# A streaming encoder step on one core: the order of the first loads (frames, rows of vectors, weights, the second block's frames)

## The chip, the cores and the metric

The kernel runs on one core of one Trainium2 chip. The metric is the device time of one execution in microseconds; of several runs the median is given. Beside it stands a profile of one execution. Its engines: TensorE (PE, with the weight loads as PEld), VectorE (DVE), ScalarE (ACT), GpSimd (POOL) and SyncE (SP), which here only issues DMAs.

## The reference

One layer of a hybrid encoder on 2048 prompt frames and 32 sample frames of 1024 channels, all float32:

```python
hn = rmsnorm(h, g_mix)
proj = hn @ w_in                       # 1024 x 3072: hA, bA, cA, zA, vB, zB of 512 columns each
yA = bA * causal_conv3(cA * hA) * silu(zA)
yB = pool_mix(vB) * silu(zB)           # trailing means over 2, 4, 8, 16 frames, a linear map, a scale
h = h + concat(yA, yB) @ w_out
gate = sigmoid(rmsnorm(h, g_ple) @ w_ple_gate)
y = rmsnorm(h + (p @ w_ple) * gate, g_final)
```

It also returns the last rows of u = cA * hA and of vB as states.

## The kernel before

**Tiling.** The 2080 frames are cut into five blocks of 416 columns (NB): three tiles of 128 frames and one short tile of 32. A tile is loaded (`x_load`, L405), its squares are summed on ScalarE (`sumsq`, L91), GpSimd makes the root (`rstd_of`, L69), VectorE normalizes it, TensorE transposes it (`turn`, L426), and what comes out of PSUM is split in two: ScalarE casts the upper part (hi), VectorE subtracts it for the lower part (lo). A product is three matmuls a piece: hi by hi, hi by lo, lo by hi. Weights of `w_in` are split in the same way: `raw_weight` (L524) loads 1024 x 128 columns, 512 KB, in pieces of 512 bytes, and casts and subtractions make hi and lo.

**The beginning** is written out by hand for the first block, with an order that the scheduler must keep where `in_turn` or `later=True` stands. SyncE first issues g_mix's row, the three frame tiles of the first block (L628) and the short tile, which holds the last 32 frames of block 0 and of block 1 in two loads (L629). `first_normal` (L634) normalizes by halves, with g_mix spread over the partitions in two PSUM tiles, `pg`, and not yet in the SBUF tile g_bc. `first_hi` and `first_lo` (L659, L663) write the pieces. VectorE's order is fixed: tile 0 and tile 1 normalized, the first lo piece, tile 2 and the short tile normalized, one hi piece, then the lo pieces. `fill` (L388) puts idle transposes on TensorE in between.

**The first weights** are zb, v and c of the first 128 columns: zb loaded at L689, v and c in `other_first` (L706). `first_products` (L599) runs three rounds of 24 matmuls over the three of them (hi by hi, hi by lo, lo by hi), and steps `second_block` (L726) forward in between. That generator takes block 1's three tiles (`x_tile`, L731: load and squares), normalizes them with g_bc (L424), transposes them, splits them into B's pieces "12" and "22" and forms the sums of blocks that the later groups' products need (T1, T2, T3, and T4, which goes to memory).

**The rows.** Small vectors (conv weights and bias, pool scale, the two caches, g_ple) are loaded as rows of one tile (L768 to L775, six loads), transposed once (L777) and kept as `vec`. Then pool_w is loaded and split (L788). The tile's memset is GpSimd's.

**Queues and buffers.** All these loads go through SyncE's one queue in the order of issue. Completion is told by eight semaphores taken in turn, so a load is issued once the load eight places ahead of it has landed. Frame tiles live in a pool of five buffers (`xin`), raw weights in one of four (`raws`: zb, v, c, pool_w; raw_h of `weights("h", ...)`, the next one, takes zb's buffer when VectorE has read it). What is not fixed by hand is put in order by a scheduler when the program is built: each engine has one list and works through it strictly in order.

SyncE's list in the beginning: g_mix, tiles 0, 1, 2, short tile (two), zb, v, c, six rows, pool_w, block 1's tiles 0, 1, 2, raw_h, raw_za, raw_b, raw_zbv.

Of the kernel before, what the change touches and what calls it, by code (L numbers as in the profile page):

```python
# [15 lines left out]
P = 128  # L16
D = 1024
KC = D // P
# [16 lines left out]
def trunk(ctx, tc, x_p, x_s, c_conv, c_pool, p_p, p_s, g_mix, w_in, conv_w, conv_b, pool_w,  # L35
          pool_scale, w_out, g_ple, w_gate, w_ple, g_fin, y_p, y_s, sc_p, sp_p, sc_s, sp_s):
    nc = tc.nc
# [53 lines left out]
    def sumsq(x, n, name, r=None, later=False):  # L91
        ssq = sm.tile([P, 1], F32, tag="ssq", name=f"ssq_{name}")
        ins = nc.scalar.activation(junk[:n], x[:n], AF.Square, accum_out=ssq[:n])  # L93
        if later:
            tc.keep_in_program_order(ins)
        return rstd_of(ssq, n, name, r)
# [207 lines left out]
    def slot(name):  # L304
        return acts[0].tile([P, SLOT], F32R, tag="hn", name=name)
# [13 lines left out]
    def ring4(t, name):  # L319
        return t.tile([P, D], F32, tag="t", name=name)  # L320
# [21 lines left out]
    with ExitStack() as s1:  # L342
# [21 lines left out]
        def ftile(name):  # L364
            return wk.tile([P, KH, P], F32, tag="f", bufs=4, name=name)
# [33 lines left out]
        def x_rows(tb, c):  # L399
            r = tb * NB + c * P  # L400
            if c < 3:
                return x_p[r:r + P]
            return x_p[r:r + DEC] if tb < 4 else x_s

        def x_load(name, rows):  # L405

            t, at = ring4(xin, f"xt_{name}"), 0
            for src in rows:
                m = src.shape[0]
                nc.sync.dma_start(t[at:at + m], src)  # L410
                at += m
            return t, at, f"x{name}"

        def x_stat(x, later=False):

            t, n, name = x
            return t, n, sumsq(t, n, name, later=later)

        def x_tile(name, rows):
            return x_stat(x_load(name, rows))  # L420

        def normal(x):
            xt, n, r = x
            nc.vector.scalar_tensor_tensor(xt[:n], xt[:n], r[:n], g_bc[:n], op0=ALU.mult, op1=ALU.mult)  # L424

        def turn(x, half, name, get=tbank, later=False):  # L426
            xt, n, _ = x
            pt = get(name)
            for k in range(KH):
                kk = half * KH + k  # L430
                ins = nc.tensor.transpose(pt[:, k * P:k * P + n], xt[:n, kk * P:(kk + 1) * P], ident[:n, :n])
                if later:
                    tc.keep_in_program_order(ins)
            return pt.rearrange("p (k t) -> p k t", k=KH)[:, :, :n]
# [68 lines left out]
        def six(g):  # L503

            B = {}
            for i, names in enumerate(SLOTS):
                t = slot(f"B{g}_{i}")
                B.update((q, piece_of(t, c)) for c, q in enumerate(names))
            return B
# [11 lines left out]
        raw_ring = lambda name: raws.tile([P, KC, P], F32, tag="t", name=name)  # L521
        spare_ring = lambda name: xin.tile([P, KC, P], F32, tag="t", name=name)

        def raw_weight(kind, j, name, ring=raw_ring):  # L524
            t = ring(f"raw_{name}")
            col = cols[kind] * WA + j * P
            raw_loads.append(nc.sync.dma_start(t, w_in[:, col:col + P].rearrange("(k p) n -> p k n", p=P)))
            return t

        raw_loads = []  # L530
# [95 lines left out]

        B0 = {}
        ahead0 = [x_load(f"0_{c}", [x_rows(0, c)]) for c in range(3)]  # L628
        short0 = x_load("0_3", [x_rows(0, 3), x_rows(1, 3)])  # L629
        B0.update(six(0))  # L630
        def in_turn(ins):
            tc.keep_in_program_order(ins)
# [26 lines left out]
        def first_hi(c, half, copy=nc.scalar.copy):  # L659
            hi, _, src = place0(c, half)  # L660
            in_turn(copy(hi, src))
# [9 lines left out]
                fill((2, 3, 2)[c], short_bank)  # L671


        for c in range(3):
            first_x.append(x_stat(ahead0[c], True))
        first_tile(0)
# [9 lines left out]
        first_hi(2, 0)  # L686
        first_tile(3)
        first_hi(2, 1, nc.vector.tensor_copy)
        raw = raw_weight("zb", 0, "firstzb")  # L689
        first_zb = [wtile(f"w_firstzb_{half}") for half in range(2)]  # L690
        for half, t in enumerate(first_zb):
            in_turn(nc.scalar.copy(t[:, :, 0], raw[:, half * KH:half * KH + KH]))
# [11 lines left out]
        first_los = {}  # L704

        def other_first(kind):  # L706
            raw = raw_weight(kind, 0, f"first{kind}")
            ts = [wtile(f"w_first{kind}_{half}") for half in range(2)]
            for half, t in enumerate(ts):
                nc.scalar.copy(t[:, :, 0], raw[:, half * KH:half * KH + KH])  # L710

            def los():
                for half, t in enumerate(ts):
                    nc.vector.tensor_tensor(t[:, :, 1], raw[:, half * KH:half * KH + KH], t[:, :, 0].bitcast(F32),
                                            op=ALU.subtract)

            first_los[kind] = los
            return ts

        first_w.extend(other_first(kind) for kind in ("v", "c"))  # L720
        for half in range(2):
            nc.scalar.copy(g_bc[:, half * NH:half * NH + NH], pg[half])
# [3 lines left out]
        def second_block():  # L726

            spans = [(c, slice(c * P, min(NB, c * P + P))) for c in range(4)]
            xs = []
            for c in range(3):  # L730
                x = x_tile(f"1_{c}", [x_rows(1, c)])  # L731
                normal(x)
                xs.append((x, slice(0, P)))
                yield
            xs.append((short0, slice(DEC, 2 * DEC)))
            whole = []
            for c, cs in spans:
                x, ts = xs[c]

                turned = x[0].rearrange("p (k t) -> p k t", k=KC)[:, :, :ts.stop - ts.start]  # L740
                for half, q in enumerate(("12", "22")):
                    pt = turn(x, half, f"pt1_{c}_{half}", bank)[:, :, ts]
                    put(B0[q][:, :, :, cs], pt)
                    nc.scalar.copy(turned[:, half * KH:half * KH + KH], pt)
                whole.append((turned[:, :KH], turned[:, KH:]))
                yield
            op = lambda o, a, b, op=ALU.subtract: nc.vector.tensor_tensor(o, a, b, op=op)
            for c, cs in spans:
                p12, p22 = whole[c]
# [12 lines left out]
                to_memory(p_d["T4"], f"T4_0_{c}", t4, c * P, n)  # L762
                yield

        second = second_block()


        rows = ftile("rows").rearrange("p k n -> p (k n)")[:112, :P]  # L768
        nc.gpsimd.memset(rows, 0.0)
        nc.sync.dma_start(rows[0:12], conv_w[0].rearrange("r (j c) -> (r j) c", c=P))  # L770
        nc.sync.dma_start(rows[12:16], conv_b[0].rearrange("(j c) -> j c", c=P))
        nc.sync.dma_start(rows[16:20], pool_scale[0].rearrange("(j c) -> j c", c=P))
        nc.sync.dma_start(rows[32:40], c_conv[0, 0].rearrange("r (j c) -> (r j) c", c=P))
        nc.sync.dma_start(rows[40:100], c_pool[0, 0].rearrange("r (j c) -> (r j) c", c=P))
        nc.sync.dma_start(rows[100:108].rearrange("k (q c) -> k q c", q=4), g_ple[0].rearrange("(q k c) -> k q c", q=4, k=KC))  # L775
        pv = tbank("pv")
        nc.tensor.transpose(pv[:, :112], rows, ident[:112, :112])  # L777
        vec = const.tile([P, 112], F32, name="vec")
# [492 lines left out]
        for gi, tbs in enumerate(GROUPS):  # L1271
            if gi == 2:

                frames_in.close()
                t = slot("hn_4")
# [40 lines left out]
    with ExitStack() as s2:  # L1316
# [113 lines left out]
        for i in range(0, NT - 1, 2):  # L1430
            with tc.issue_after(loaded[-1].ins):
                x = [load_rows(xh, "x", i + b, x_p) for b in range(2)] if i else [first_x, second_x]
# [4 lines left out]
            if last:  # L1437
                n = tiles[NT - 1][1]
# [6 lines left out]
            if last:  # L1445
                x = load_rows(xh, "x", NT - 1, x_p, x_s)
# [34 lines left out]
        for k in range(KH):  # L1481
            raw = [ring4(t, f"wg_r{k}_{i}") for i, t in enumerate(((ya, ya), (ya, xh), (xh, xh), (ya, ya))[k])]
# [243 lines left out]
        n = tiles[NT - 1][1]  # L1726
# [47 lines left out]
```

## Time and profile before

| what | us |
|---|---|
| median of 3 runs | 921.37 |
| lowest and highest | 920.61, 921.42 |
| the profiled execution | 921.02 |
| its span in the profile | 919.2 |
| mean granted TensorE clock in the span | 0.997 |

How the views read. The stages give, for each stretch of the span, the busy time and number of instructions of PE, PEld, DVE, ACT and POOL, then the granted clock, the share of the DMA engines and GB/s. The chain of waits is the work that ended last, followed back: start, duration, engine, tile or group and line. The timeline gives start, busy time, engine, line, operation, output and inputs, shapes, count, and in brackets the idle time just ahead with what ended it. "SPq" is SyncE's queue: its time is the issue, not the transfer. In the list of DMA issues the last number is the time from issue to landing. Line numbers are those of the kernel before.

### The profile page before, as it was taken

The page shows a single profiled execution, that of the slowest core. Times are in us where ns is not written, and L with a number is a line of the kernel's source. Part 1 is how long each engine was busy: PE and PEld are TensorE (multiplying, and loading weights), DVE is VectorE, ACT ScalarE, POOL GpSimd, SP SyncE. Part 2 cuts the span into 40 slices and gives each one's busy share as a digit, 9 for nine tenths or more (in the row PEclk, how much of TensorE's full clock was granted, in tenths as well). Part 3 has the DMA queues.
Part 4 walks back from the last instruction along what each step waited for, and adds up shares of the span by engine and source line. Part 5 has one row for each costly group of instructions (what it writes and reads, how often), then busy time and mean ns, then how long its engine had stood idle before and what let it go on. Part 6 is the DMA issues. An engine that isn't in the chain of part 4 may idle for free.

```text
span 919.2 us, 13202 instructions
## 1 busy us (share of the span) xinstructions
PE 905.7 (99%) x4529; PEld 822.7 (90%) x4529; DVE 722.4 (79%) x1236; ACT 481.2 (52%) x894; POOL 159.8 (17%) x307
## 2 busy tenths in 40 slices
PE   8999999999999999999999999999999999999996
PEld 6999999999999999999999987888878878888885
DVE  6996989999576989795777679665558658889885
ACT  7744565654445555443545356334336755555554
POOL 3111222121000333210000120111203301111113
PEclk9999999999999999999999999999999999999998
DMA  9357687798945898638975469865777984676564
GB/s 262 93 145 217 168 249 230 234 294 287 413 131 168 251 227 225 216 122 296 274 228 173 155 243 291 267 189 177 237 228 231 354 263 143 203 242 235 188 209 169
DMA packets 138447, 205.12 MB, mean 223 GB/s; under 512 B 13116, under 2 KB 101724, under 8 KB 137101
## 3 DMA queue, kind: packets, MB, share of 16 engines
q1 hardware_dynamic: 117773, 139.41, 48.9%
q0 software_dynamic: 17872, 59.45, 19.8%
q10 hardware_dynamic: 2736, 5.44, 1.8%
q8 instruction: 35, 0.57, 0.3%
q14 instruction: 31, 0.25, 0.1%
HBM read 136.60 MB, written 67.64 MB: 222 GB/s over the span
## 4 chain that ended last, share of the span: by engine, by line
PE 91%; DVE 3%; DMA 2%; ACT 2%; issue 1%; POOL 0%; SPq 0%; POOLq 0%; DVEq 0%; ACTq 0%
PE x_g L175 9%; PE x_o L175 9%; PE x_zab L591 7%; PE x_zbv L591 6%; PE x_ch L591 5%; PE z_g L175 5%; PE e L107 4%; PE z_o L175 4%; PE z_zab L591 3%; PE h L591 3%; PE z_zbv L591 3%; PE z_ch L591 3%; PE b L591 3%; PE za L591 3%; PE zb L591 2%; PE c L591 2%
## 5 line engine op out<-in xcount | busy, mean ns | idle before, releaser
L80 ACT CAST y_S<-y_fS 128x512 fp32r<-128x512 f32 x32 | 19.5, 622 | 42.2 <-PE x_o L175 20.4
L175 PE MATMUL x_g<-wg_b,g_S 128*128 128x512 f32 x128 | 35.7, 389 | 0.0
L175 PE MATMUL x_o<-wo_b,y_S 128*128 128x512 f32 x128 | 35.6, 390 | 0.0
L591 PE MATMUL x_zab<-B,w_zab_S 128*128 128x416 f32 x168 | 34.2, 352 | 0.2 <-ACT V L987 0.2
L591 PE MATMUL z_zab<-B,w_zab_S 128*128 128x416 f32 x168 | 34.3, 351 | 0.0
L591 PE MATMUL x_zbv<-B,w_zbv_S 128*128 128x416 f32 x168 | 34.2, 352 | 0.0
L591 PE MATMUL z_ch<-B,w_ch_S 128*128 128x416 f32 x168 | 34.1, 351 | 0.0
L591 PE MATMUL z_zbv<-B,w_zbv_S 128*128 128x416 f32 x168 | 34.0, 351 | 0.0
L591 PE MATMUL x_ch<-B,w_ch_S 128*128 128x416 f32 x168 | 34.0, 351 | 0.0
L107 PE MATMUL e<-wq,pps 128*128 128x512 f32 x144 | 33.1, 390 | 0.0
L591 PEld LDWEIGHTS x_zab<-B,w_zab_S 128*128 128x128 f32 x168 | 31.3, 188 | 0.9 <-ACT V L987 0.5
L107 PEld LDWEIGHTS e<-wq,pps 128*128 128x128 f32 x144 | 27.0, 188 | 5.6
L591 PEld LDWEIGHTS z_zbv<-B,w_zbv_S 128*128 128x128 f32 x168 | 31.4, 188 | 0.3
L591 PEld LDWEIGHTS x_ch<-B,w_ch_S 128*128 128x128 f32 x168 | 31.4, 188 | 0.3
L591 PEld LDWEIGHTS z_ch<-B,w_ch_S 128*128 128x128 f32 x168 | 31.3, 188 | 0.3
L591 PEld LDWEIGHTS z_zab<-B,w_zab_S 128*128 128x128 f32 x168 | 31.3, 188 | 0.3
L591 PEld LDWEIGHTS x_zbv<-B,w_zbv_S 128*128 128x128 f32 x168 | 31.3, 188 | 0.4
L1542 DVE SCALAR_TENSOR_TENSOR h<-h,rstd_f,g_bc 128x1024 f32<-128x1024 f32 (+1 forms) x15 | 19.3, 1284 | 14.0 <-POOL rstd_f L76 14.0
L80 ACT CAST y<-y 128x512 fp32r<-128x512 f32 x24 | 14.8, 618 | 29.4 <-PE z_o L175 12.8
L1335 DVE TENSOR_TENSOR c_o<-x_o,x 128x512 f32<-128x512 f32 x14 | 9.7, 691 | 25.7 <-PE x_o L175 25.7
L72 POOL TENSOR_SCALAR ms_f<-ssq_f 128x1 f32<-128x1 f32 (+1 forms) x15 | 6.6, 441 | 128.8 <-ACT junk L93 128.5
L175 PEld LDWEIGHTS x_o<-wo_b,y_S 128*128 128x128 f32 x128 | 23.9, 188 | 5.2 <-ACT c_o L1340 0.3
(591 smaller groups left out, 2694.9 us busy)
## 6 DMA issues: line engine op xcount, KB each, us to landing
y<-y_d SPq DMA_DIRECT2D x16, 512.0 KB, 6.0
x<-in_x_prompt_dram SPq DMA_DIRECT2D x16, 512.0 KB, 6.0
h_d<-x SPq DMA_DIRECT2D x16, 512.0 KB, 4.3
h<-h_d SPq DMA_DIRECT2D x16, 512.0 KB, 3.5
xt<-in_x_prompt_dram SPq DMA_DIRECT2D x15, 512.0 KB, 7.8
e<-e_d SPq DMA_DIRECT2D x15, 512.0 KB, 5.2
out_dram<-h POOLq DMA_DIRECT2D x14, 512.0 KB, 3.0
p_dT<-T POOLq DMA_DIRECT2D x12, 512.0 KB, 6.0
```

What stands on the lines that cost most here:

```text
L72: nc.gpsimd.tensor_scalar(ms[:n], ssq[:n], scalar1=1.0 / D, scalar2=EPS, op0=ALU.mult, op1=ALU.add)
L80: ins = nc.scalar.copy(hi, src)
L107: nc.tensor.matmul(ps, pps[:, a, k], wp[k][b][:, cs], start=k + q == 0, stop=k == 1 and q == 2)
L175: nc.tensor.matmul(ps[:n], lhs[:, k, a, :n], w[b][:, k], start=start and k + q == 0, stop=k == KH - 1 and q == 2, skip_group_check=True)
L591: nc.tensor.matmul(ps[:, :NB], lhs[:, k, x], b[:, k, y], start=start and k + q == 0, stop=stop and k == KH - 1 and q == 2, skip_group_chec ...
L1335: add = lambda o, a, b: nc.vector.tensor_tensor(o, a, b, op=ALU.add)
L1542: nc.vector.scalar_tensor_tensor(h[:n], h[:n], rf[:n], g_bc[:n], op0=ALU.mult, op1=ALU.mult)
```

## The change

- The three frame tiles' loads are kept in a list, and `third_landed` is the third one's load.
- The rows' tile, its memset and five of its six loads move up, to right behind the frames' loads. The sixth (g_ple) stands behind block 1's first tile.
- The loads of zb, v and c are issued together, behind them. zb's gets an added dependency on the third frame tile's load.
- Block 1's first tile is loaded right behind c; tiles 1 and 2 are loaded when v and c are made, ahead of pool_w. `second_block` takes the tiles so loaded instead of loading them.

```diff
+        frame_loads = []
...
-                nc.sync.dma_start(t[at:at + m], src)
+                frame_loads.append(nc.sync.dma_start(t[at:at + m], src))
...
-        def raw_weight(kind, j, name, ring=raw_ring):
+        def raw_weight(kind, j, name, ring=raw_ring, behind=None):
...
+            if behind is not None:
+                tc.add_manual_dep(raw_loads[-1].ins, behind.ins.name, mybir.DependencyInfo(
+                    mybir.DependencyClass.Sync, mybir.DependencyReason.DATA), reason="leaves the bandwidth to frames")
...
         ahead0 = [x_load(f"0_{c}", [x_rows(0, c)]) for c in range(3)]
+        third_landed = frame_loads[-1]
         short0 = x_load("0_3", [x_rows(0, 3), x_rows(1, 3)])
+
+        rows = ftile("rows").rearrange("p k n -> p (k n)")[:112, :P]
+        nc.gpsimd.memset(rows, 0.0)
+        nc.sync.dma_start(rows[0:12], conv_w[0].rearrange("r (j c) -> (r j) c", c=P))
...
+        nc.sync.dma_start(rows[40:100], c_pool[0, 0].rearrange("r (j c) -> (r j) c", c=P))
...
+        first_raws = {kind: raw_weight(kind, 0, f"first{kind}", behind=third_landed if kind == "zb" else None)
+                      for kind in ("zb", "v", "c")}
+        with tc.issue_after(raw_loads[-1].ins):
+            ahead1 = [x_load("1_0", [x_rows(1, 0)])]
+        nc.sync.dma_start(rows[100:108].rearrange("k (q c) -> k q c", q=4), g_ple[0].rearrange("(q k c) -> k q c", q=4, k=KC))
...
-        raw = raw_weight("zb", 0, "firstzb")
+        raw = first_raws["zb"]
...
-            raw = raw_weight(kind, 0, f"first{kind}")
+            raw = first_raws[kind]
...
+        ahead1 += [x_load(f"1_{c}", [x_rows(1, c)]) for c in range(1, 3)]
         first_w.extend(other_first(kind) for kind in ("v", "c"))
...
-                x = x_tile(f"1_{c}", [x_rows(1, c)])
+                x = x_stat(ahead1[c])
...
-        rows = ftile("rows").rearrange("p k n -> p (k n)")[:112, :P]
-        nc.gpsimd.memset(rows, 0.0)
```

The six loads of the rows go from their old place behind `second`. In the built program this also moves instructions that the diff does not name. On SyncE: g_mix, tiles 0, 1, 2, short tile (two), five rows, zb, v, c, block 1's tile 0, the sixth row, block 1's tiles 1 and 2, pool_w, raw_h. On ScalarE: the two copies of g_bc go from behind c's casts to ahead of zb's; pool_w's cast goes from ahead of the squares of block 1 to behind them, and the first half of raw_h's cast follows it, ahead of block 1's pieces instead of behind the first two. On VectorE: pool_w's and half of raw_h's remainders stand ahead of block 1's pieces. TensorE's order stays nearly as it was, and from about 75 us on the lists of all engines are in the same order as before.

More of the change, by code (lines that the diff above doesn't have):

```diff
@@ L628, in trunk @@
         ahead0 = [x_load(f"0_{c}", [x_rows(0, c)]) for c in range(3)]
+        third_landed = frame_loads[-1]
         short0 = x_load("0_3", [x_rows(0, 3), x_rows(1, 3)])
+        rows = ftile("rows").rearrange("p k n -> p (k n)")[:112, :P]
+        nc.gpsimd.memset(rows, 0.0)
+        nc.sync.dma_start(rows[0:12], conv_w[0].rearrange("r (j c) -> (r j) c", c=P))
+        nc.sync.dma_start(rows[12:16], conv_b[0].rearrange("(j c) -> j c", c=P))
+        nc.sync.dma_start(rows[16:20], pool_scale[0].rearrange("(j c) -> j c", c=P))
+        nc.sync.dma_start(rows[32:40], c_conv[0, 0].rearrange("r (j c) -> (r j) c", c=P))
+        nc.sync.dma_start(rows[40:100], c_pool[0, 0].rearrange("r (j c) -> (r j) c", c=P))
         B0.update(six(0))
@@ L765, in trunk @@
         second = second_block()
-        rows = ftile("rows").rearrange("p k n -> p (k n)")[:112, :P]
-        nc.gpsimd.memset(rows, 0.0)
[L770 to L775, printed above, removed]
         pv = tbank("pv")
```

## The prediction

> **What bounds the kernel now.** I read the page's busy shares first, then the stages of the beginning, then the chain of waits, then the instructions in order of time.
>
> ```profile
> span 919.2 us, 13202 instructions
> ...
> PE 905.7 (99%) x4529; PEld 822.7 (90%) x4529; DVE 722.4 (79%) x1236; ACT 481.2 (52%) x894; POOL 159.8 (17%) x307
> ```
>
> TensorE is the bound. A change in the beginning can only move the moment from which its work runs without a hole. The stages (PE, PEld, DVE, ACT, POOL busy, granted clock, DMA share, GB/s) show when that is:
>
> ```profile
> 0.00:12.00 12.00, 9.27 (x36) 5.88 (x36) 5.22 (x10) 7.48 (x14) 4.81 (x45) 1.00 0.90 240
> 12.00:14.70 2.70, 1.69 (x14) 1.28 (x14) 2.69 (x5) 2.70 (x8) 0.00 (x0) 1.00 0.98 231
> 14.70:24.20 9.50, 9.45 (x51) 9.28 (x52) 9.38 (x16) 6.71 (x13) 3.69 (x6) 1.00 0.97 302
> 24.20:33.40 9.20, 8.81 (x60) 7.84 (x59) 8.03 (x17) 8.36 (x19) 0.61 (x1) 1.00 0.43 114
> 33.40:75.00 41.60, 41.60 (x222) 41.17 (x222) 38.81 (x76) 19.16 (x39) 3.60 (x4) 1.00 0.44 125
> ```
>
> Up to 14.7 there is no product; from 14.7 to 24.2 and from 33.4 on, TensorE has no hole; between 24.2 and 33.4 it has small ones (weight loads 7.84 of 9.20). DMA is nearly full until 24. So a gain must make the first product earlier than 14.7 or fill the holes of 24 to 33. The chain of waits says what the first product and the restart hang on:
>
> ```profile
> 12.01 1.40 DVE xt L639 x2
> 13.40 0.60 DVE B L661
> 14.01 0.61 DVE B L665
> 14.75 1.75 PE zb L619 x8
> ...
> 26.63 0.52 ACT zs L907
> ...
> 32.61 0.46 PE zb L591
> 33.73 4.34 PE zb L591 x23
> ```
>
> The first product hangs on VectorE (normalizing, then the pieces of the frames), not on a weight. The timeline of those engines:
>
> ```profile
> 5.00 1.06 ACT L93 ACTIVATE junk<-xt 128x1024 bf16<-128x1024 f32 x1 [2.79 <-DMA xt<-in_x_prompt_dram]
> ...
> 6.39 1.06 ACT L93 ACTIVATE junk<-xt 128x1024 bf16<-128x1024 f32 x1 [0.24 <-DMA xt<-in_x_prompt_dram]
> ...
> 7.10 2.80 DVE L639 SCALAR_TENSOR_TENSOR xt<-xt,rstd_x,gm 128x512 f32<-128x512 f32 x4 [4.92 <-POOL rstd_x L76]
> ...
> 8.24 1.06 ACT L93 ACTIVATE junk<-xt 128x1024 bf16<-128x1024 f32 x1 [0.69 <-DMA xt<-in_x_prompt_dram]
> ...
> 9.89 0.69 DVE L665 TENSOR_TENSOR B<-pt,B 128x512 fp32r<-128x512 f32 x1
> ...
> 10.50 2.90 DVE L639 SCALAR_TENSOR_TENSOR xt<-xt,rstd_x,gm 128x512 f32<-128x512 f32 x4
> ...
> 10.99 2.00 ACT L661 CAST B<-pt 128x512 fp32r<-128x512 f32 x4
> ...
> 12.88 1.15 ACT L692 CAST w_firstzb<-raw_firstzb 128x512 fp32r<-128x512 f32 x2
> ...
> 13.96 0.43 ACT L661 CAST B<-pt 128x128 fp32r<-128x128 f32 x2
> ...
> 14.27 1.15 ACT L710 CAST w_firstv<-raw_firstv 128x512 fp32r<-128x512 f32 x2
> ...
> 14.72 1.43 PEld L619 LDWEIGHTS zb<-B,w_firstzb 128*128 128x128 f32 x8 [0.94 <-ACT B L661]
> ...
> 16.36 1.08 ACT L722 COPY g_bc<-gm 128x512 f32<-128x512 f32 x2
> 17.31 0.65 ACT L80 CAST pw<-raw_pw 128x512 fp32r<-128x512 f32 x1
> ...
> 18.70 1.06 ACT L93 ACTIVATE junk<-xt 128x1024 bf16<-128x1024 f32 x1 [0.74 <-DMA xt<-in_x_prompt_dram]
> ```
>
> Once the first tile's root is there (7.10), VectorE has no hole to speak of until 14.6, and its order is fixed by hand. The third tile makes ScalarE wait 0.69 us (8.24), but VectorE has older work then: only its piece at 9.89 waits a little for ScalarE, by at most the 0.1 to 0.3 us by which that copy sits behind the late square. This is all that an earlier third tile can give the first product.
>
> **The change part by part.** The loads, with SyncE's issues of before:
>
> ```profile
> 3.48 0.46 SPq L527 DMA_DIRECT2D raw_firstzb<-in_w_in_dram  x1
> ...
> 5.07 4.29 SPq L527 DMA_DIRECT2D raw_firstc<-in_w_in_dram  x1
> ...
> 15.04 1.37 SPq L410 DMA_DIRECT2D xt<-in_x_prompt_dram  x3
> ...
> 18.66 0.38 SPq L527 DMA_DIRECT2D raw_h<-in_w_in_dram  x1
> ```
>
> ```profile
> SPq L410 <- DMA raw_firstc<-in_w_in_dram: 1.5, 1, 1.5
> ```
>
> Each load of this queue waits for the landing of the load eight places before it; the row of waits shows it for the second block's first tile, eight places behind weight c. With five loads of rows ahead of them, the weights zb, v and c are eight places behind the third tile and the two halves of the short one. So the added wait costs nothing of its own: place alone makes zb wait for the third tile. Behind zb on SyncE stand v, c, the second block's first tile, the last row load, its other two tiles, pool_w and raw_h. The five row loads cost SyncE five issues of at most 0.4 us (the small issues above) while it would wait anyway; GpSimd's memset keeps its place.
>
> When does zb land? The third tile lands between one spacing of the first two (ScalarE starts their squares at 5.00 and 6.39, so 7.8) and the 8.2 of before; without weights in the queue I take 7.8. A 512 KB weight from issue to landing:
>
> ```profile
> raw_ch_2a<-in_w_in_dram SPq DMA_DIRECT2D x2, 512.0 KB, 3.7
> ```
>
> ```profile
> raw_firstv<-in_w_in_dram SPq DMA_DIRECT2D x1, 512.0 KB, 9.2
> ...
> raw_b<-in_w_in_dram SPq DMA_DIRECT2D x1, 512.0 KB, 7.6
> ```
>
> 3.7 us is a load with little ahead of it, 7.6 and 9.2 are loads deep in a full queue. I take 3.7, since the queue has drained by then: zb at 11.6, bounds 11.5 and 15.4 (7.8 + 7.6). v of before landed at 13.2 (issue at 3.98 + 9.2) and c at 15.0 (the row of waits), so 1.85 us per weight: v at 13.5, c at 15.3, close to before.
>
> The Trainium skill, page "DMA: Bandwidth & Descriptors", section "Anatomy of one DMA", speaks against the change: about 2.0 us of fixed cost plus bytes at 436 GB/s per transfer, paid in the open when a queue drains. By it zb would land at an estimated 11.0 and the sum would not change; the trace agrees in kind (3.7 us alone against 1.85 us in a stream).
>
> The order on ScalarE is what costs. In the new program the two copies of g_bc stand ahead of the zb casts instead of behind c's, and each waits for VectorE's last reading of its half (normalizing the short tile; the block of four that began at 10.50 ends at 13.40). So:
> - second g_bc copy from 13.45; the next instruction starts 0.48 us on (16.36 to 17.31 is 0.95 for two): 13.93;
> - two zb casts, 1.08 us start to start of what follows (12.88 to 13.96): 15.01;
> - the first copy of the short tile, 0.27 us of the pair's 0.43, and 0.1 us to TensorE (14.62 to 14.72 before): 15.38.
>
> Against 14.72 that is +0.66; with VectorE 0.1 to 0.3 us earlier, **+0.4 to +0.6, taken +0.45**. zb has 2.3 us of slack (needed at 13.93), v 1.9 (needed at 15.4), c 1.2 (16.5).
>
> From the first product to 24.2 TensorE is full; all is shifted. Next are the second block's tiles. The first is issued when c's issue is through: 7.9 + 0.46 + 1.05 + 4.29 = 13.7 at the latest; plus 3.66 (15.04 to 18.70), 17.4. ScalarE is ready for its square at about 17.1 (c's casts end there; g_bc and pool_w's cast, 1.0 and 0.6 us, are gone from this place), so the squares come about 1.3 us earlier. That buys nothing by itself: the tiles are first transposed behind the second round of products.
>
> ```profile
> 24.67 1.08 ACT L80 CAST B<-pt 128x512 fp32r<-128x512 f32 x2 [2.10 <-PE pt L431]
> ...
> 25.63 0.63 ACT L80 CAST w_h<-raw_h 128x512 fp32r<-128x512 f32 x1
> ```
>
> In 24 to 33 the two engines that feed TensorE trade work. ScalarE takes the first raw_h cast ahead of the second block's pieces, into idle time of before (2.10 us ahead of 24.67, the rows above), and one copy later, but one cast of a T piece earlier: about -0.5. VectorE takes raw_h's remainder (far later before) and one difference ahead of the last pieces, 0.6 us each (the piece at 14.01): +1.2, of which I let its earlier work on the second block's tiles, ready some 0.9 us sooner, give back most. So the stage's length stays within 0.5 us either way; I take +0.15. After 33.4 TensorE is full and orders differ only in work with slack.
>
> Sum: +0.45 +0.15 = **+0.6 us**. On the profiled execution (921.02 us, of which 1.82 us lie outside the span) 921.6; the median of the runs shown is 0.35 us higher, 921.37, so **922.0 us**.
>
> **The rivals.**
> 1. *It works as worded: the frames' wait was worth its idle time.* For it: 0.69 us before the third square, 0.74 us at 18.70, holes in 24 to 33. Against it: VectorE, not ScalarE, leads to 14.6. If the g_bc copies did not delay (VectorE through 0.5 us sooner), -0.5: 920.9. The most, 0.24 + 0.69 of ScalarE's waits and about 0.7 of the holes, is -1.6: 919.8. Chance 0.12; 0.04 of it beyond -0.2%, which takes that most and the runs' spread (921.37 to 920.61) together.
> 2. *The weights become the bound (slower).* They are asked for some 4.4 us later than before. Each us that zb lands after 13.93 delays the first product by one, as each of c after about 17.5 delays the third. At raw_b's 7.6 us zb lands at 15.4: +0.6 +1.5 = 923.5; at raw_firstv's 9.2, 925.1. Against it: the queue is empty then. Chance 0.15, of it 0.12 past +0.2%.
> 3. *raw_h leads.* Its cast stands ahead of the second block's pieces now. It starts at 25.63 before, right behind other work, so raw_h has landed by then; needed now by about 24.9, each us later costs one. Issued at 18.7 again, 3.7 us give 22.4, 7.6 us 26.3: +0.6 +1.4 = 923.4. Chance 0.08, of it 0.06 past +0.2%.
> 4. *The clock falls back.* TensorE idles 0.94 us ahead of the first product, here some 1.4. Early transposes took 0.22 us each, later ones 0.13:
>
> ```profile
> 7.90 1.76 PE L431 MATMUL pt<-ident,xt 128*128 128x128 f32 x8
> ...
> 9.72 1.04 PE L431 MATMUL pt<-ident,xt 128*128 128x128 f32 x8
> ```
>
> The slow stretch shown is 1.8 us long; if the clock fell back for one to two such stretches at half speed, 0.9 to 1.8 us of work would be lost: with the +0.6 up to 923.8. Against it: the hole of 0.94 us before did not slow the first products (1.75 us for eight). Chance 0.03. The Trainium skill, "TensorE: Matmul & The Clock Gate", Part 1, has the clock halve after an idle window of about 3.4 us; by that rule 1.4 us would not do it.
>
> **How the numbers follow.** Forecast 0.62 (921.4 to 922.8), rivals 0.12, 0.15, 0.08, 0.03. A measurement of this kernel can tell about 0.2%, 1.84 us, from no change. Faster by more: 0.04. Slower by more: 0.12 + 0.06 + 0.03 = 0.21. Within: 0.62 + 0.08 + 0.03 + 0.02 = 0.75. The range takes in the forecast, the first rival's usual size and half of the second and third: 920.4 to 924.2.
>
> **What would show it.** The added wait is idle on SyncE ahead of zb until about 7.8; zb's casts start near 13.9 right behind g_bc with no DMA wait; TensorE's first product is at 15.1 to 15.4; the second block's first square is near 17.1; the restart is near 33.1, and from there all is shifted by about 0.6. A first product before 14.7, a DMA wait ahead of the zb casts, or a DMA wait ahead of raw_h's cast would make the prediction wrong.

## The result, and the profile after

The changed kernel takes 924.03 us (median of 22 runs, 922.18 to 928.03) against 921.76 us (22 runs, 920.10 to 924.14) of the kernel before on the same chip: a ratio of 1.0026, with a 95% interval of 1.0016 to 1.0035, so +2.4 us (1.5 to 3.2). On another chip it was 923.73 against 922.72 us, 1.0012 (1.0000 to 1.0023), +1.1 us (0 to 2.1). The forecast was 922.0 us, +0.6 us: the time is within its range, but the likeliest case was too small, and in the first of the two comparisons the loss is past the 0.2% that, in the prediction, a measurement can tell from no change.

The profiled execution took 925.9 us. The page of the changed kernel begins:

```profile
span 924.1 us, 13204 instructions
...
PE 907.9 (98%) x4529; PEld 823.7 (89%) x4529; DVE 721.3 (78%) x1236; ACT 480.8 (52%) x894; POOL 161.1 (17%) x307
```

The stages of the changed kernel (PE, PEld, DVE, ACT and POOL busy, granted clock, DMA share, GB/s):

```profile
0.00:12.00 12.00, 8.51 (x32) 5.36 (x32) 4.08 (x9) 6.36 (x12) 4.10 (x43) 1.00 0.61 188
12.00:14.70 2.70, 2.12 (x17) 1.61 (x18) 2.70 (x5) 2.70 (x7) 0.73 (x2) 1.00 1.20 302
14.70:24.20 9.50, 8.14 (x38) 7.80 (x37) 8.58 (x16) 7.91 (x17) 4.17 (x6) 0.82 1.04 328
24.20:33.40 9.20, 9.03 (x59) 8.56 (x58) 7.79 (x12) 5.16 (x11) 0.61 (x1) 1.00 0.47 135
33.40:75.00 41.60, 41.38 (x223) 40.22 (x222) 39.69 (x81) 21.28 (x45) 3.61 (x4) 1.00 0.39 121
```

Three things differ from before. DMA is idle more in the first 12 us (share 0.61, before 0.90): weight zb waits. VectorE does less there (4.08 us, before 5.22). And from 14.7 to 24.2 TensorE does 38 matmuls instead of 51, at a granted clock of 0.82. The clock was 0.51 from 16.2 to 19.6 (the same view and columns):

```profile
16.20:19.60 3.40, 3.31 (x10) 3.20 (x11) 3.40 (x9) 3.33 (x8) 0.00 (x0) 0.51 1.01 395
19.60:23.00 3.40, 3.40 (x20) 3.33 (x19) 2.48 (x6) 2.81 (x5) 3.13 (x4) 1.00 0.97 286
```

Ten matmuls in 3.40 us, where the next 3.40 us have twenty. So 3.4 us ran at half speed, and 1.7 us of work was lost.

The chain of waits of this profile begins only behind this stage, so the timeline is read in its place. The timeline of the changed kernel ahead of the first product (start, duration, engine, line, operation, tiles, count; in brackets the engine's idle time before it and what ended it):

```profile
9.36 0.40 SPq L529 DMA_DIRECT2D raw_firstzb<-in_w_in_dram  x1
9.42 1.06 ACT L93 ACTIVATE junk<-xt 128x1024 bf16<-128x1024 f32 x1 [1.73 <-DMA xt<-in_x_prompt_dram]
...
11.08 0.69 DVE L679 TENSOR_TENSOR B<-pt,B 128x512 fp32r<-128x512 f32 x1 [1.04 <-ACT B L675]
...
11.68 2.73 DVE L653 SCALAR_TENSOR_TENSOR xt<-xt,rstd_x,gm 128x512 f32<-128x512 f32 x4
...
13.89 1.15 ACT L744 COPY g_bc<-gm 128x512 f32<-128x512 f32 x2
...
14.94 1.14 ACT L713 CAST w_firstzb<-raw_firstzb 128x512 fp32r<-128x512 f32 x2
...
15.97 0.43 ACT L675 CAST B<-pt 128x128 fp32r<-128x128 f32 x2
...
16.29 0.85 PEld L624 LDWEIGHTS zb<-B,w_firstzb 128*128 128x128 f32 x3 [1.50 <-ACT B L675]
```

The third tile, for which the weights now wait, came later, not earlier: ScalarE waits 1.73 us for it and squares it at 9.42 (before 8.24). VectorE's piece behind that square starts at 11.08 after 1.04 us of idle (before 9.89, without a gap). The copies of g_bc stand ahead of the zb casts, which follow without a DMA wait. The first product is at 16.29, 1.57 us later than before.

Where the time went in this profile: +1.57 at the first product; from there to the restart (the first product of the second block) 19.36 us instead of 17.89, +1.47, of which the clock's 1.7 is all and more. The last weight load of product b is at 77.60 (before 74.37, +3.2), and another 1.7 us come later. In the second profile of the changed kernel these four are +0.73, +1.52, +2.4 and +0.4: the rest of the kernel varies from one execution to the next.

### The profile page after: what moved, and what is told of

Its sections match the earlier page's. It is cut to its first block, busy times and chain, and to the rows that moved or that the text cites. A ratio compares the mean times of both kernels' runs of the same rounds, so it can differ in the third digit from the quotient of the medians.

```text
span 924.1 us, 13204 instructions
## 1 busy us (share of the span) xinstructions
PE 907.9 (98%) x4529; PEld 823.7 (89%) x4529; DVE 721.3 (78%) x1236; ACT 480.8 (52%) x894; POOL 161.1 (17%) x307
## 4 chain that ended last, share of the span: by engine, by line
PE 78%; DVE 5%; DMA 3%; issue 1%; ACT 1%; POOL 0%; POOLq 0%; DVEq 0%; ACTq 0%
PE x_g L175 9%; PE x_o L175 8%; PE x_zab L596 6%; PE z_g L175 5%; PE x_zbv L596 5%; PE e L107 4%; PE x_ch L596 4%; PE z_o L175 4%; PE z_zab L596 3%; PE z_zbv L596 2%; PE z_ch L596 2%; PE y_g L175 2%; PE y_o L175 2%; PE za L596 2%; PE b L596 2%; PE h L596 2%
```

## The experiments

Each was timed against the kernel before on its own chip (922.6 to 922.7 us there; 921.76 for the row "changed"). This table gathers what the profiles show; all times in us. "Square" is the start of the third square on ScalarE, right behind the landing of the third tile; "first" is the first product, and "diff." the time between the two; "hole" is from the start of TensorE's last weight load ahead of the first product to the start of its own; "fall" is when the clock went to 0.5 in the beginning, for 3.4 us each time; "restart" is the first product of the second block, and "behind first" its distance from the first product. Differences were taken before rounding. Two of the profiles have a further fall far behind the beginning: at 156.6 (g_bc ahead) and at 740.5 (wait alone).

```
kernel                      square  first  diff.  hole  fall   restart  behind first  ratio (95%)
before                       8.24   14.72  6.48   1.08   -     32.61    17.89
before again                 8.30   14.60  6.31   1.08   -     32.47    17.87
wait alone                   8.46   14.77  6.31   1.08   -     33.46    18.68   1.0002 (0.9990-1.0013)
rows back                    9.08   15.39  6.31   1.08   -     34.65    19.26   1.0010 (1.0002-1.0019)
no wait                      9.81   16.22  6.41   1.08   -     34.68    18.45   1.0009 (0.9997-1.0020)
g_bc behind                  9.37   15.69  6.32   1.08  35.74  35.66    19.98   1.0026 (1.0016-1.0035)
pieces first                 9.32   15.63  6.31   1.08   -     35.79    20.15   1.0020 (1.0007-1.0032)
changed                      9.42   16.29  6.87   1.64  16.15  35.65    19.36   1.0026 (1.0016-1.0035)
changed again                8.57   15.45  6.88   1.63  16.33  34.86    19.41   1.0012 (1.0000-1.0023)
rows alone                   8.75   15.62  6.87   1.64  15.80  35.13    19.51   1.0012 (1.0003-1.0021)
g_bc ahead, loads of before  9.18   16.05  6.87   1.64  16.62  35.01    18.96   1.0024 (1.0014-1.0034)
fill in the hole             9.14   16.01  6.87   0.50   -     34.97    18.96   1.0041 (1.0027-1.0055)
fill too late                9.56   16.92  7.35   0.11   -     35.40    18.48   1.0026 (1.0013-1.0038)
short tile behind            8.64   16.56  7.92   1.07  16.45  35.45    18.89   1.0025 (1.0016-1.0034)
```

**The changed kernel again.** No edit.

> The changed kernel once more, unaltered, to see what of its profile recurs. Theory A (the five row loads, which stand right behind the frames, hold the third tile back): the third square starts again near 9.4 instead of 8.24, the first product near 16.3. Theory B (the third tile was late by chance in that one execution): the third square is back at 7.8 to 8.3 and the first product at 15.1 to 15.4. Theory C (TensorE's two holes of 1.6 us ahead of the first product let its clock fall to one half for 3.4 us, which costs 1.6 us): a hole of 1.6 us comes with a clock of 0.5 from about 16.2 and first eight products of 3.1 us instead of 1.75; without the hole there is no fall. Median 2 to 3 us above the kernel before by A with C, 0.3 to 0.9 by B alone.

Measured: square at 8.57, first product at 15.45, a hole of 1.63 and a fall at 16.33; +1.1 us. The landing varies by 0.85 us between two executions of one kernel, so chance (B) is part of it. C's sign recurred: the eight weight loads of v took 2.63 us instead of 1.51.

**The rows alone.**

```
         short0 = x_load("0_3", ...)
+        rows = ftile("rows")... ; memset; five loads of rows
 ...
-        rows = ftile("rows")... ; memset; five loads of rows
         nc.sync.dma_start(rows[100:108]..., g_ple...)
```

> The kernel before with only the five row loads moved ahead of the weights (the sixth, the second block's frames and the weights' place in the program stay; by the ring of eight semaphores weight zb still waits for the third tile). Theory A: the third square near 9.4, the first product near 16.3, and with C the clock at 0.5 for 3.4 us: +2 to +3 us on the kernel before, the same as the whole change. Theory B: third square at 7.8 to 8.3, first product 15.1 to 15.4 because the copies of g_bc stand ahead of the zb casts here too: +0.3 to +0.9.

Measured: square at 8.75, hole 1.64, fall at 15.80, 1.0012. Up to the first product it has the changed kernel's order on ScalarE, and it has its time.

**The rows back.** The changed kernel with all six row loads where they were.

> The changed kernel with all six row loads back at their old place; the added wait of weight zb for the third tile and the second block's early frames stay. ScalarE's order then has the copies of g_bc behind c's casts again. Theory A: third square at 7.8 to 8.2, first product at 14.2 to 14.8, clock at 1.0 all through: -0.6 to +0.2 us on the kernel before. Theory B says nothing against that. Theory W (it is the wait that costs, weights come too late): first product still at 15.5 or later behind a DMA wait of the zb casts, +1 us or more.

Measured: the third tile is late again (square at 9.08) with no row load near it, so A isn't needed for a late tile. First product at 15.39, no fall; yet the restart is 19.26 behind it, and the time is 1.0010. W's DMA wait did not occur.

**The copies of g_bc behind.**

```
-            nc.scalar.copy(g_bc[...], pg[half])
+            in_turn(nc.scalar.copy(g_bc[...], pg[half]))
```

> The changed kernel with one order fixed: the two copies of g_bc on ScalarE keep their place behind the zb casts and the short tile's copies, as in the kernel before; all loads as changed. Theory O (the order on ScalarE is what delays the first product): zb casts start when zb lands (12 to 13.4), the first product comes 0.5 us (third tile in time) to 1.3 us (third tile late) earlier than in the changed kernel, at about 14.7 to 15.0. With theory C the hole ahead of it shrinks to about 0.4 us, the clock stays at 1.0 and another 1.6 us are saved: 0 to +0.7 us on the kernel before. If O is wrong the time stays 2 to 3 us above the kernel before.

Measured: the hole is 1.08 again and the first product 0.56 nearer to the third square, as O says. But the time did not fall (1.0026): the restart came 19.98 behind the first product, after a hole of 1.87 us, and the clock fell there, at 35.74.

**The kernel before again.** No edit.

> The kernel before once more, unaltered, for a second profile of it: does the third frame tile land near 8.2 again, with the weights' packets in the queue behind it? Theory W (the frames' last packets come in later when nothing stands behind them in the queue, so the wait harms the tile that it was meant for): 7.8 to 8.3, against 8.5 to 9.3 in the five profiles with the wait. Theory B (chance): anything from 7.8 to 9.3. First product 14.5 to 15, no fall of the clock.

Measured: square at 8.30, first product at 14.60. The timeline shows what the first profile of it had not:

```profile
8.30 1.06 ACT L93 ACTIVATE junk<-xt 128x1024 bf16<-128x1024 f32 x1 [1.39 <-DMA xt<-in_x_prompt_dram]
...
9.95 0.69 DVE L665 TENSOR_TENSOR B<-pt,B 128x512 fp32r<-128x512 f32 x1 [0.69 <-ACT B L661]
```

Here VectorE had begun at 6.46 instead of 7.10, and it does wait, 0.69 us, for the work behind the third tile.

**No wait.** The changed kernel with the three weights asked for right behind the frames, the rows behind them.

> The changed kernel with the three weights asked for right behind the frames, as in the kernel before, and the five row loads behind the weights: no wait for the third tile by hand or by place; the second block's frames early as changed. ScalarE's order then has the copies of g_bc behind c's casts by itself. Theory W: third square near 8.2, zb landed near 11.5, first product at 14.5 to 14.9, no fall of the clock, -0.5 to +0.7 us on the kernel before. Theory D (it is the other order of work in the stage of 24 to 33 that costs): first product at 14.7 but the restart behind 34, +1 to +2 us.

Measured: the latest third tile of all (square at 9.81), with the weights' packets behind it in the queue. So W falls too: what stands behind the tile does not order these landings. Restart 18.45 behind the first product, 1.0009.

**The wait alone.**

```
-        raw = raw_weight("zb", 0, "firstzb")
+        raw = raw_weight("zb", 0, "firstzb", behind=frame_loads[2])
```

> The kernel before with nothing but the wait: weight zb asks for its data once the third frame tile has landed; every engine's order of instructions is that of the kernel before. Theory W: third square later than 8.24, zb landed at 12 to 13.3, first product at 15.0 to 15.5, in some executions a fall of the clock: +0.5 to +1.5 us. The prediction's step (the wait costs nothing of its own, zb has slack): zb at 11.6 to 12, first product at 14.5 to 14.9, within 0.3 us of the kernel before.

Every engine's order is that of before. Its timeline:

```profile
8.40 0.39 SPq L529 DMA_DIRECT2D raw_firstzb<-in_w_in_dram  x1
8.46 1.06 ACT L93 ACTIVATE junk<-xt 128x1024 bf16<-128x1024 f32 x1 [1.61 <-DMA xt<-in_x_prompt_dram]
...
12.94 1.15 ACT L697 CAST w_firstzb<-raw_firstzb 128x512 fp32r<-128x512 f32 x2
...
14.77 0.48 PEld L624 LDWEIGHTS zb<-B,w_firstzb 128*128 128x128 f32 x3 [0.94 <-ACT B L666]
```

zb is asked for 4.9 us later than before, and its casts still have no DMA wait. The time is 1.0002 (0.9990 to 1.0013): the wait costs nothing that can be told, and gives nothing: the third tile came at 8.4, no earlier than with the weights in the queue. In this profile the restart was 0.8 us further behind the first product than before, since the last tile of the second block landed at 23.2 instead of 21.3; over all twelve runs no such loss is seen.

**Fill too late.** The changed kernel with ten transposes of the identity ahead of the first product.

> The changed kernel with ten more transposes of the identity on TensorE between the short tile's transposes and the first product, into the bank that the product then overwrites; some 0.13 us each, 1.1 to 1.3 us of the hole of 1.6 us. Theory C (the hole makes the clock fall): no fall of the clock ahead of 24, the first eight products take 1.75 us and not 3; the first product stays at 15.4 to 16.3; in the profile 1.6 us less at the end of b's products than in the changed kernel (about 75.2 to 76), in the median 0.5 to 1.6 us less, as only some executions fall. Without C: no change, or some 0.1 us more.

They went into the bank that the first product overwrites, and VectorE's piece released them only at 15.87, so they ran behind the hole, which was 1.08 us for them, and delayed the product to 16.92. No fall; 1.0026. It tells little of C, but it points to something else that the first product waits for, its own bank.

**Fill in the hole.** The same ten, into the bank of the first g_bc copy:

```
         for half in range(2):
             nc.scalar.copy(g_bc[...], pg[half])
+        fill(10, pg[0])
```

> The changed kernel with ten transposes of the identity in the hole of 1.64 us ahead of the first product, now into the bank of the first g_bc copy, which is free by then (the fills before had to wait for a bank that VectorE frees only at the first product's own start). Everything else stands in the changed kernel's order. Theory C (the hole lets the clock fall in some six of ten executions, 1.6 us each): no fall ahead of 24 in the profile, the end of b's products 18.9 + 42.4 us behind the first product as in the kernels without a fall, the mean granted clock of the runs back near 0.998 from 0.997, and the median some 1 us less than the changed kernel's, so +0.3 to +1.2 us on the kernel before. Without C: +1.5 to +2.4 us as the changed kernel, and a clock of 0.997.

Measured, in its timeline:

```profile
14.58 1.31 PE L391 MATMUL gm<-ident 128*128 128x128 f32 x10
...
16.01 1.06 PEld L624 LDWEIGHTS zb<-B,w_firstzb 128*128 128x128 f32 x6 [0.36 <-ACT B L675]
...
34.55 0.54 ACT L80 CAST B<-pt 128x128 fp32r<-128x128 f32 x2
...
34.97 0.19 PEld L596 LDWEIGHTS zb<-B,w_firstzb 128*128 128x128 f32 x1 [1.44 <-ACT B L80]
```

and in its stage:

```profile
14.00:24.20 10.20, 10.07 (x61) 9.50 (x60) 9.22 (x18) 8.07 (x17) 4.55 (x4) 1.00 1.07 328
```

The clock held, as C says. The gain did not arrive: TensorE now waits 1.44 us ahead of the restart for the last pieces, which comes 18.96 behind the first product, as late as with a fall. The time, from five runs, is 1.0041 (1.0027 to 1.0055), no better than the changed kernel's.

**The order alone.** The kernel before, loads untouched, with g_bc's copies ahead of the zb casts:

```
         raw = raw_weight("zb", 0, "firstzb")
+        for half in range(2):
+            in_turn(nc.scalar.copy(g_bc[...], pg[half]))
```

> The kernel before, its loads untouched, with the two copies of g_bc put ahead of the zb casts on ScalarE. Theory O: the hole ahead of the first product is 1.64 us instead of 1.08, so the first product is 0.56 us later (near 15.2). With C the clock falls in some of the executions (mean granted clock near 0.997): +1 to +2 us in the median, without any of the moved loads. If O is right and C wrong: +0.5 us. If both are wrong: no change.

Measured, in its timeline:

```profile
9.18 1.06 ACT L93 ACTIVATE junk<-xt 128x1024 bf16<-128x1024 f32 x1 [2.13 <-DMA xt<-in_x_prompt_dram]
...
13.65 1.15 ACT L691 COPY g_bc<-gm 128x512 f32<-128x512 f32 x2
...
14.69 1.14 ACT L694 CAST w_firstzb<-raw_firstzb 128x512 fp32r<-128x512 f32 x2
...
16.05 1.43 PEld L619 LDWEIGHTS zb<-B,w_firstzb 128*128 128x128 f32 x6 [1.50 <-ACT B L661]
```

The clock behind it:

```profile
16.65:20.00 3.35, 3.35 (x12) 3.19 (x11) 2.71 (x6) 3.00 (x6) 0.00 (x0) 0.50 0.96 345
```

The hole is 1.64, the clock falls, the time is 1.0024 (1.0014 to 1.0034), +2.2 us: as much as the whole change, without one moved load. The third tile was late here too, with the loads of before. But the two copies are not all that moved in the built program. ScalarE's order between 27 and 35 is another than before, and VectorE does raw_h's remainder and one difference ahead of the second block's last pieces, as in the changed kernel:

```profile
29.37 0.68 DVE L83 TENSOR_TENSOR w_h<-raw_h,w_h 128x512 fp32r<-128x512 f32 x1
...
32.97 0.69 DVE L747 TENSOR_TENSOR f<-f,B 128x512 f32<-128x512 f32 x1
...
34.14 1.68 DVE L83 TENSOR_TENSOR B<-pt,B 128x512 fp32r<-128x512 f32 x4
```

So what was tested alone is the order of the engines' work as a whole, not the place of the two copies.

**The short tile behind.** The kernel before with the short tile's loads meant to wait for the third tile.

> The kernel before with the two halves of the short tile asked for once the third tile has landed (and with them, as they stand ahead on SyncE, the weights). Theory S (the short halves write their 32 rows of 4 KB each into the same 64 partitions as eight of the sixteen engines still working on the third tile, and hold these up): the third tile lands near 7.1, all sixteen engines within 0.5 us, instead of 8.2 to 9.7 with half the engines 1 to 2 us behind. Without S it lands at 8.2 or later again. The time: the first product hangs on VectorE either way, 0 to +1 us.

Measured: inconclusive. Only one of the two halves waited; the other kept its place, and weight zb moved up right behind it. The square was at 8.64, the half that waited landed at 11.66, the first product then hung on the short tile (16.56, with a hole of 1.73 us ahead of its transposes and a fall at 16.45), and the time was 1.0025. S stays open.

**The pieces first.** The kernel of "g_bc behind", and on VectorE the four jobs put behind the second block's last piece:

```
+                with tc.issue_after(last_piece[0].ins):
                     op(t1, p12, part("11", 0)) ...
 ...
+                    with tc.issue_after(last_piece[0].ins):
                         wh = weights("h", j, f"h{tag}")
```

> The changed kernel with its loads, with the copies of g_bc behind the zb casts, and now also with VectorE's order in the stage of 24 to 33 set right: raw_h's remainder and the differences of the first piece (four jobs of 0.6 us, three of which the changed kernel's VectorE does ahead of the second block's last pieces and one more ahead of the first) stand behind the second block's last piece. Theory V (up to the restart of the products VectorE is as close to the end as TensorE; what was lost is work put ahead of the pieces on it): the restart comes 16.9 to 17.9 us behind the first product instead of 18.5 to 20.0 in the profiles without a fall of the clock, no idle of over 1 us on TensorE ahead of it, and the median is +0 to +1 us on the kernel before, 1.4 to 2.4 us less than with the copies of g_bc alone set right. Theory T (the third tile's landing decides, whatever stands behind it): the restart is 17.9 us or more behind a first product at 15.4 or later, and the median stays at +1.5 to +2.5 us.

Measured, in its timeline:

```profile
28.62 1.28 DVE L83 TENSOR_TENSOR B<-pt,B 128x512 fp32r<-128x512 f32 x2
...
29.34 0.58 ACT L768 COPY xt<-pt 128x512 f32<-128x512 f32 x1 [2.73 <-DVE B L83]
29.82 0.52 ACT L925 ACTIVATE zs<-zb 128x416 f32<-128x416 f32 x1
29.97 0.42 PEld L435 LDWEIGHTS pt<-ident,xt 128*128 128x128 f32 x4 [2.31 <-ACT xt L768]
```

V in this form falls. ScalarE's order moved with VectorE's: a copy that waits for VectorE's piece now stands ahead of other work, ScalarE idles 2.73 us, TensorE 2.31 us for the bank, and the restart is 20.15 behind the first product. 1.0020 (1.0007 to 1.0032), not to be told from the changed kernel. None of the versions run beats the kernel before.

## Why the prediction was right or wrong, point by point

**The number:** inside the range, in part by luck. The upper end, 924.2, was set by late weights and a late raw_h, and neither led. What was slow instead was a stage to which the prediction gave +0.15, and a third tile that it took to be on time.

**The added wait costs nothing of its own:** right. With the wait alone and every order kept, 1.0002; zb's casts had no DMA wait in any profile with the wait.

**The order on ScalarE costs +0.45 (0.4 to 0.6; 0.66 with nothing given back by VectorE):** right in place and size. From the third square to the first product it is 6.31 to 6.48 us in the seven profiles that keep g_bc behind and let nothing else in, and 6.87 or 6.88 in the five with g_bc ahead: 0.56. That the order alone loses as much as the whole change (1.0024 against 1.0026 and 1.0012) shows that the moved loads are not needed for the loss: the new order of the engines' work is enough. It is not the only order that loses: with g_bc behind and the changed loads it was 1.0026. What the second block's early frames cost or give with every order kept was not run. With g_bc behind, but other orders on VectorE and ScalarE, the two runs that have them took 1.0010 (rows back) and 1.0009 (no wait).

**"The first product hangs on VectorE (normalizing, then the pieces of the frames), not on a weight"**, with an earlier third tile worth 0.1 to 0.3 us: half wrong. It hangs on no weight. But the same constant difference over landings from 8.2 to 9.7 shows that it hangs on the third tile, through VectorE. The profile before was one in which VectorE began 0.64 us later than in the second profile, so that it had no idle time to show.

**The third tile at 7.8 without weights in the queue:** wrong; it landed at 8.4 to 9.5 in the profiles with a wait. What makes it late is open. By the squares it is not the rows (rows back, 9.08) and not the empty queue (no wait, 9.81); the loads of before gave 8.24, 8.30 and 9.18. Chance can give 0.85 us, yet the three earliest of fourteen are the three with every order of before.

**The stage from the first product to the restart, +0.15:** this is the term that was mis-sized. Measured: +1.47 and +1.52 in the two profiles of the changed kernel. In them the fall of the clock, with its 1.7, is enough to account for it: rival 4, which had a chance of 0.03 because a hole of 0.94 us (1.08 by the table's measure) had not slowed the first products. A hole of 1.64 us did, in four profiles of four with that hole left open. Each run lists its granted clock, a mean over the span. The mean of these is 0.9968 for the changed kernel again (12 runs) and 0.9969 for the rows alone (11), against 0.9981 for the kernel before beside them (35); and 0.9968 for the order alone (11) against 0.9977 (21). That is 0.0009 to 0.0013 of 923 us, 0.8 to 1.2 us of work, about half to two thirds of one fall, as if it came in a part of the executions. With the 0.56 that makes 1.4 to 1.8 us, an estimate to set beside the measured +1.1 and +2.4. It is a rough one: the mean also holds a clock of 0.5 at the end of every profile (from 914 on before) and falls in other places. In the 22 runs that gave +2.4 us it is 0.9972, not lower than in the 12 that gave +1.1; and with g_bc behind, where the hole ahead of the first product is closed and the fall of the profile is at 35.74, it is 0.9970. In the two kernels with the changed orders and a mean near that of before, the time didn't come back: 1.0026 with 0.9978 (fill too late), 1.0041 with 0.9974 (fill in the hole). So the runs show that the fall comes with the open hole and what it costs in a profile that has it; that it makes the loss of the median is not shown.

**But the clock is not the only leg of that term.** With the fall taken away (fill in the hole) the stage stayed at 18.96, +1.07 on the kernel before, and the kernels in which the clock did not fall ahead of the restart, the kernel before apart, took 18.45 to 20.15. The other leg is what the prediction let be given back: "+1.2, of which I let its earlier work on the second block's tiles ... give back most". VectorE in the changed kernel, in the order of its start:

```profile
27.32 0.68 DVE L83 TENSOR_TENSOR w_h<-raw_h,w_h 128x512 fp32r<-128x512 f32 x1
...
33.61 0.68 DVE L769 TENSOR_TENSOR f<-f,B 128x512 f32<-128x512 f32 x1
...
34.78 1.67 DVE L83 TENSOR_TENSOR B<-pt,B 128x512 fp32r<-128x512 f32 x4
```

Both jobs that were named stand ahead of the last pieces. What was to be given back, 0.9 us, came in small part or not at all in the two fill kernels, which have this order and no fall. In "fill in the hole" VectorE begins to normalize the second block 5.84 us behind the first product, where it was 7.21 before, but ends 11.45 behind it, before 11.40, since it waits for GpSimd's roots (two of these waits are 0.44 and 0.71 us); in "fill too late" it ends 10.98 behind. Then come pool_w's and raw_h's remainders, and the pieces start 12.57 and 12.09 behind the first product, before 11.32. ScalarE waits for them (fill in the hole):

```profile
26.18 1.28 DVE L426 SCALAR_TENSOR_TENSOR xt<-xt,rstd_x,g_bc 128x1024 f32<-128x1024 f32 x1 [0.71 <-POOL rstd_x L76]
27.38 0.69 DVE L83 TENSOR_TENSOR pw<-raw_pw,pw 128x512 fp32r<-128x512 f32 x1
27.98 0.69 DVE L83 TENSOR_TENSOR w_h<-raw_h,w_h 128x512 fp32r<-128x512 f32 x1
28.58 1.28 DVE L83 TENSOR_TENSOR B<-pt,B 128x512 fp32r<-128x512 f32 x2
...
29.30 1.18 ACT L767 COPY xt<-pt 128x512 f32<-128x512 f32 x2 [0.88 <-DVE B L83]
```

From 29.30 on ScalarE has no gap until its piece that lets TensorE restart at 34.97. From VectorE's first work to the restart (the fifth number is DVE busy), the kernel before, then the changed one:

```profile
7.10:32.61 25.51, 23.74 (x148) 21.48 (x146) 24.11 (x39) 21.12 (x46) 6.50 (x12) 1.00 0.85 224
```

```profile
7.30:35.65 28.35, 24.85 (x146) 22.47 (x146) 24.97 (x41) 20.98 (x45) 6.99 (x12) 0.94 0.69 201
```

VectorE has 24.11 us of work in 25.51 before: it is as near to the end as TensorE. Now it has 24.97, +0.86, and 3.38 us of idle instead of 1.40, the late tile's 1.04 among them. The reading is that VectorE's lateness hides behind TensorE when the clock slows that, and otherwise reaches the restart, through ScalarE, so that undoing one of the two gives nothing back. It is argued from these rows and not shown by a run: "the pieces first", which took the named jobs away from ahead of the pieces, moved ScalarE's order too and did not bring the restart forward. How the loss is shared between them in a common execution stays open: g_bc behind, fill and pieces first each removed one part, and each put the orders of other work out of place as well.

**The weights as bound, raw_h as bound:** right not to lead. A DMA wait ahead of raw_h's cast, named as a sign against the prediction, did occur in the changed kernel:

```profile
23.93 0.62 ACT L80 CAST w_h<-raw_h 128x512 fp32r<-128x512 f32 x1 [1.28 <-DMA raw_h<-in_w_in_dram]
...
27.73 1.08 ACT L80 CAST B<-pt 128x512 fp32r<-128x512 f32 x2 [3.17 <-PE pt L433]
```

It had cover: ScalarE's next work waits another 3.17 us for TensorE. Weight zb landed later than the 11.6 of the prediction, about 13.4 in this profile (issued at 9.36, 4.0 us to landing), and still ahead of its cast at 14.94.

## What to carry to other kernels

Where a scheduler orders the engines, moving a load moves the order of work that hardly touches it; compare the orders first, and test the order alone and the load alone, since here the added wait of a load was worth 0 and the order +2.2 us. A constant difference between a landing and the end, over several profiles, tells what leads, where one profile without an idle gap doesn't. When two engines are both within a microsecond or two of the end, a stall undone on one of them may show nothing until the other is mended too.

## What the runs showed of the hardware

The clock fell to one half for 3.4 us behind a hole of 1.64 us in TensorE's work, with transposes ahead of it. It did not fall behind longer holes of 2.45 us (pieces first, 27.52 to 29.97) and 1.99 us (rows back, 27.29 to 29.28), and it did behind 1.87 us (g_bc behind). So the length of one hole does not decide. The Trainium skill, page "TensorE: Matmul & The Clock Gate", Part 1, asks for an idle window of about 3.4 us, and has the window run freely: the length of the falls agrees with such a window, the idle time asked for does not. Nor does TensorE's busy time in the 3.4 us ahead decide, as the profile has it (its ends of matmuls are modelled): the changed kernel ahead of its fall, then pieces first, without a fall at the end of the stretch:

```profile
12.74:16.15 3.41, 2.09 (x18) 1.44 (x16) 3.41 (x7) 3.41 (x9) 0.25 (x1) 1.00 1.23 299
```

```profile
26.31:29.72 3.41, 1.59 (x11) 1.29 (x9) 2.91 (x4) 0.68 (x2) 0.47 (x1) 1.00 0.11 27
```

What decides stays open.

A small operation on GpSimd lasted as long as the VectorE operation beside it. In the kernel with the wait alone, the mean of a tile (128x1) takes 0.19 us at 9.70, with VectorE idle, and 1.29 us here, beside VectorE's normalizing of the tile before (24.48 to 25.77):

```profile
24.53 1.29 POOL L72 TENSOR_SCALAR ms_x<-ssq_x 128x1 f32<-128x1 f32 x1
25.90 0.55 POOL L76 TENSOR_TENSOR rstd_x<-ms_x,nhalf 128x1 f32<-128x1 f32 x1
```

VectorE's next normalizing then waits for the root:

```profile
26.48 1.28 DVE L426 SCALAR_TENSOR_TENSOR xt<-xt,rstd_x,g_bc 128x1024 f32<-128x1024 f32 x1 [0.72 <-POOL rstd_x L76]
```

Normalizing three tiles in such a chain has waits of 0.44, 0.71 and 0.72 us; in the kernel before, with two roots ready ahead, it has the one of 0.44.
